# Unread matmuls at the start, page rows moved ahead of four products, pooling tiles moved into the input stage, last rows two steps sooner: a decoder trunk on one core

## The chip, the cores and the metric

The kernel runs on one core of a Trainium2 chip. The metric is the device time of one execution in microseconds, as the median of several executions. Profiled executions also give a span, from the first to the last instruction, and a trace of every engine: TensorE (PE; PEld is its weight load), VectorE (DVE), ScalarE (ACT), GpSimd (POOL) and SyncE (SP), whose queue issues all transfers here.

## The reference

One step of a two-layer decoder trunk for a prompt of 512 tokens and 8 sample sequences of 4 tokens, 544 columns in all, model width 1024. All tensors are fp32.

```
h = rmsnorm(x, g_mix);  z = h @ w_in      # one projection, split into:
    u_pool, q, kv (6 streams), nsa_gate, c_b, c_c, c_x, gate_pool, gate_nsa, gate_conv
y_pool = pool_mixer(u_pool)               # trailing means over 2/4/8/16 tokens, minus the token, then a map
y_nsa  = nsa_mixer(q, kv, nsa_gate)       # compressed + selected + windowed attention, rope on q and k
         # kv of the samples' past: cache_kv[l][page_table], 16 pages of 128 rows
y_conv = c_b * conv3(c_c * c_x)
merged = sum over b: sigmoid(gate_b) * (y_b @ w_br_b);   x = x + merged @ w_out
x = x + (silu(conv3(h2 @ W_a)) * (h2 @ W_b)) @ W_down    # h2 = rmsnorm(x, g_ffn)
after both layers: y = rmsnorm(x, norm_final)
```

## The kernel before

Activations lie transposed, 128 features by 544 columns, in tiles for each 128 features. A product tile (128 output features) is a Task in a list that is the same for both layers. It is computed in two halves of 272 columns; each half takes, for each of 8 k-tiles, three matmuls (L323, L324, L326: weight high part by input high part, high by low, low by high), 24 in all, 48 a task. A weight tile is fetched by SyncE (L306, `wr`), cast to its high part `wh` by ScalarE (L298) and its residual `wl` taken by VectorE (L299). The residual of the inputs of the first product comes from L1225. Product halves land in PSUM buffers `pg` of which there are three; a task's `evac` reads them.

The order on TensorE is the order in which the program is written. The other engines' orders are laid out by the framework's scheduler at build time, each engine then runs its own list in order.

A layer has stages. Stage "z" (the input products) holds in this order: zkc, zvc, zks (compressed keys and values, selected keys; these three run together behind the first normalisation, `mode="norm"`), zkw (window keys), four query tiles zq, zvs, zvw, zng (attention's gates), and parts of the convolution and of the compression. Keys and queries are rotated in `z_rope`: ScalarE copies PSUM to a tile (L481), SyncE shuffles it with four transfers (L483), GpSimd multiplies (L485), VectorE multiplies and adds (L484, L486); keys are then cast by ScalarE into a stacked tile (L495). A task can carry `pre`, code emitted ahead of its evacuation or product: `pages(a)` emits `pages_some` (two transfers a page, L455, with a page number loaded from memory in SyncE, L443). All pages must be there for `cmp_split`, whose casts on ScalarE are L532 and whose residuals are L534.

Behind "z" comes attention, in which TensorE's program interleaves units of one head, one branch (selected, windowed) and one block of 128 queries with tasks of stage "fill": gates and branch products of the convolution and the pooling mixer (L1085, L1093). `self.fill` says how many microseconds of fill follow a unit. A unit is scores (L830), mask, maximum, exponent (L844, L846, L852), scaling by the gate (L859 on GpSimd), transposition on TensorE (L872) and a split (L874, L875); `head_out` (L910) multiplies by the values and, for a pair of heads, splits the result (L915, L916, L341, L342) for the branch product "n" behind the attention. The pooling tiles zpool (`pool`: `pool_mix`, then `pool_map` some half products later) stand in the fill.

At the end the last down products are summed per half of the columns (L1238, L1246); `final_rows(hf)` computes the rows' factor (L374 to L393) and multiplies (L1262 on GpSimd, L1264 on VectorE). `later(n, fn)` runs a function n half products on; `fl[1]` is that number for `final_rows(0)`.

Of the kernel before, what the change touches and what calls it, by code (L numbers as in the profile page):

```python
# [6 lines left out]
F32 = mybir.dt.float32  # L7
F32R = mybir.dt.float32r
# [8 lines left out]
NP = 512  # L17
# [199 lines left out]
class Task:  # L217
    def __init__(self, name, evac, w, x, m, pre, mode, stage, halves, keep):
        self.name, self.evac, self.w, self.x, self.m = name, evac, w, x, m
        self.pre, self.mode, self.stage, self.halves, self.keep = pre, mode, stage, halves, keep  # L220
# [1 line left out]


class Trunk:
    def __init__(self, tc, ins, outs, ctx, slots=49, work=8, fill=1.66, look=3, lag=3, np_=4, nps=2, pm=9, ng=3, raw=3, by_pool=((0, 1, 2, 3, 4, 5, 6, 7), (1, 3, 5)), fl=(2, 7, 6, 1), ys=(4.0, 3.0, 10.0, 3.0, 3.0, 3.5)):
        self.tc, self.nc, self.i, self.o = tc, tc.nc, ins, outs
        pool = lambda name, **k: ctx.enter_context(tc.tile_pool(name=name, **k))
        self.cp = pool("cp", bufs=1)
        self.wp = pool("wp", bufs=4)
        self.bp = pool("bp", bufs=3)  # L230
        self.tp = pool("tp", bufs=slots)
        self.kp = pool("kp", bufs=work)
        self.dp = pool("dp", bufs=1, space=bass.MemoryType.DRAM)
        self.sp = pool("sp", bufs=2)
        self.ps = pool("ps", bufs=1, space=bass.MemoryType.PSUM)
        self.n = 0
        self.ng, self.raw = ng, raw
        self.by_pool, self.fl, self.ys_ = by_pool, fl, ys
        self.np_, self.nps, self.pm = np_, nps, pm
        self.fill, self.look, self.lag = fill, look, lag  # L240


    def nm(self, p):
# [155 lines left out]
    def setup(self):  # L399
        nc, i = self.nc, self.i  # L400
        self.cst = self.cp.tile([128, CS_W], F32, name="cst")
        self.norms = self.cp.tile([128, NM_W], F32, name="norms")
        self.ones = self.cp.tile([128, 2], F32, name="ones")
        self.vc = self.cp.tile([128, 256], F32R, name="vc").rearrange("p (g n) -> p g n", g=2)
        self.cT = self.cp.tile([128, 512], F32R, name="cT")
        self.ptt = self.cp.tile([1, 16], I32, name="ptt")
        self.cst1 = self.cst2 = None
        nc.vector.memset(self.ones, 1.0)
        nc.scalar.activation(self.ones[:, 1:2], self.ones[:, 0:1], AF.Tanh)
        self.x = [self.T() for _ in range(KT)]  # L410
        self.ident = self.c("ident")
        nc.gpsimd.memset(self.vc[64:128].bitcast(F32), 0.0)
        nc.gpsimd.memset(self.cT[64:128].bitcast(F32), 0.0)
        s, v, g = nc.scalar, nc.vector, nc.gpsimd
        by = ((s, None), (s, v), (g, None), (s, v), (s, v), (g, g), (s, v), (s, v))
        ap = self.tl[0].w[0]
        r = self.raw_weights(8)
        for t, a in ((self.norms, i["norms"]), (self.x[0], i["xT"][:, 0]), (r[:, 0:4], ap[:, 0:4]),
                     (self.x[1], i["xT"][:, 1]), (r[:, 4:8], ap[:, 4:8])):
            nc.sync.dma_start(t, a)  # L420
        for k in range(2, 7):
            nc.sync.dma_start(self.x[k], i["xT"][:, k])
        self.norm_tile(0, 0, "g_in")
        w = self.weight_parts(r, 0, 4)
        self.norm_tile(1, 0, "g_in")
        self.got[0] = w + self.weight_parts(r, 4, 8)
        self.nxt = 1
        for k in range(2, 7):
            self.norm_tile(k, 0, "g_in")
        for k in range(3):  # L430
            self.square_sum(self.x[k], k, *by[k])
        self.ahead(2)
        nc.sync.dma_start(self.x[7], i["xT"][:, 7])
        nc.sync.dma_start(self.cst, i["cst"])
        nc.sync.dma_start(self.ptt, i["pt"])
        for u in range(3, 7):
            self.square_sum(self.x[u], u, *by[u])
        self.norm_tile(7, 0, "g_in")
        self.square_sum(self.x[7], 7, *by[7])
# [522 lines left out]
    def tasks(self, l):  # L962
        nc, i = self.nc, self.i
# [3 lines left out]
        def add(name, evac, w, x=h, m=128, pre=None, mode=None, stage="rest", halves=(0, 1), keep=None):  # L967
            T.append(Task(f"{name}.{l}", evac, w, x, m, pre, mode, stage, halves, keep))

        def zt(m):  # L970
            return (i["w_in"][l, m], 8)
# [31 lines left out]
        def raw_kv(j):  # L1003
            def evac(ps):
                if j == 0:
                    nc.gpsimd.tensor_mul(self.cosr, self.cosr, self.r)
                    nc.gpsimd.tensor_mul(self.sinr, self.sinr, self.r)
                z = self.z_raw(ps)
                store("kvT", j, z)
                self.cmp_prompt(j, z)  # L1010
            return evac

        add("zkc", raw_kv(0), zt(0), pre=begin, mode="norm", stage="z")
        add("zvc", raw_kv(1), zt(1), stage="z")
        pages = lambda a: lambda: self.pages_some(l, range(a, min(a + 3, 16)))

        def rope_k(name, out, j, off, e0):
            def evac(ps):
                z = self.z_rope(ps)
                store(out, j, z)  # L1020
                setattr(self, name, self.k_stack(z, off))
                nc.gpsimd.tensor_copy(self.E[:, :, e0:e0 + 4], self.seq4(z))
            return evac

        add("zks", rope_k("ksel", "kvT", 2, 32, 16), zt(2), pre=pages(0), stage="z")
        add("zkw", rope_k("kwin", "wT", 0, 0, 20), zt(3), pre=pages(3), stage="z")

        def rope_q(r):
            def evac(ps):
# [2 lines left out]
                    self.sample_prep()  # L1032
            return evac

        for r in range(4):
            add("zq", rope_q(r), zt(4 + r), pre=pages(6 + 3 * r), stage="z")

        def raw_v(name, out, j, e0):
            def evac(ps):
# [61 lines left out]
                    nc.gpsimd.tensor_add(self.mg[m], self.mg[m], t)  # L1101
            return evac

        def pool(j):
            def evac(ps):
                pd = self.pool_mix(j, ps)
                for hf in range(2):
                    self.later(self.pm + hf, lambda hf=hf: self.pool_map(j, pd, hf))
            return evac

        kinds = {"c": (18, 0, lambda: self.yc), "p": (26, 2, lambda: self.yp), "n": (34,)}
        seq = [(key, m) for key in "cp" for m in range(8)]
        for n, (key, m) in enumerate(seq + [("n", 0)]):
            if n == 6:
                for j in range(2):
                    add("zpool", pool(j), zt(16 + j), stage="fill")
            add("gate", gate(key, m), zt(kinds[key][0] + m), stage="fill")
            if n > 0:
                key, m = seq[n - 1]
                k0, x = kinds[key][1:]  # L1120
                add("branch", branch(key, m), (i["br_a"][l, m, :, k0:k0 + 2], 2), x=x, stage="fill")
# [303 lines left out]
```

## Time and profile before

| | |
|---|---|
| median of three runs | 1762.97 us (1758.93, 1762.97, 1764.65) |
| profiled execution, its own time | 1759.85 us |
| its span | 1758.0 us |
| mean granted TensorE clock | 0.993 of full speed |
| busy: TensorE, VectorE, ScalarE, GpSimd | 1710.2, 1145.0, 737.2, 487.4 us |

An engine's busy time counts its instructions, not its waits. In a timeline a row gives the start and the duration of one instruction or of several merged, and in brackets the idle time of the engine ahead of it and what ended it. The granted clock 1.00 stands for 2.4 GHz and 0.50 for 1.2 GHz.

### The profile page before, as it was taken

What the parts mean: (1) busy time and instruction counts of PE and PEld (TensorE: products, weight loads), DVE (VectorE), ACT (ScalarE), POOL (GpSimd) and SP (SyncE); (2) the same over time, 40 slices, a digit from 0 to 9 for tenths busy, and PEclk for the clock granted to TensorE, in tenths of its full rate; (3) what the DMA queues carried; (4) which work ended last, traced back from release to release, by engine and by line L of the source; (5) the groups of instructions that cost most, each with busy time, mean ns of one, the idle gap of its engine ahead of it and who ended that gap; (6) DMA issues with size and microseconds to landing.
All of it is one profiled execution on the core that took longest, in us unless ns stands there. A gap on an engine that the chain in (4) does not pass through costs nothing.

```text
span 1758.0 us, 35101 instructions
## 1 busy us (share of the span) xinstructions
PE 1710.2 (97%) x13488; PEld 1689.6 (96%) x13488; DVE 1145.0 (65%) x2552; ACT 737.2 (42%) x1499; POOL 487.4 (28%) x719
## 2 busy tenths in 40 slices
PE   8999989999999999999998998999999999999996
PEld 8999989999999999999998998999999999999996
DVE  6675888856566565565857568887564665565566
ACT  5443555643333233233435345666333333232333
POOL 3212655630122121121231226456001321121113
PEclk9999999999999999999999999999999999999998
DMA  6653211224222322322465532112242222323322
GB/s 216 178 183 113 68 47 46 64 78 150 89 85 74 107 77 86 100 77 77 152 176 148 186 116 49 46 49 64 78 153 90 86 83 91 91 79 97 91 75 78
DMA packets 97208, 175.52 MB, mean 100 GB/s; under 512 B 31250, under 2 KB 51858, under 8 KB 97042
## 3 DMA queue, kind: packets, MB, share of 16 engines
q1 hardware_dynamic: 97042, 173.29, 32.5%
q8 instruction: 107, 1.75, 0.4%
q14 instruction: 59, 0.48, 0.1%
HBM read 157.19 MB, written 12.71 MB: 97 GB/s over the span
## 4 chain that ended last, share of the span: by engine, by line
PE 87%; DVE 7%; SPq 2%; DMA 2%; ACT 1%; issue 1%; POOL 0%; DVEq 0%; ACTq 0%; POOLq 0%
PE pg L323 25%; PE pg L324 25%; PE pg L326 25%; PE ps L830 2%; PE po L910 2%; PE pt L872 2%; SPq L483 1%; SPq L455 1%; DVE mx L846 1%; PE ps L323 1%; PE ps L324 1%; PE ps L326 1%; PE ps L1328 1%; PE ps L1329 1%; PE ps L1330 1%
## 5 line engine op out<-in xcount | busy, mean ns | idle before, releaser
L323 PE MATMUL pg<-t,wh 128*128 128x272 f32 x3824 | 1122.1, 294 | 19.8 <-DVE t L1093 8.3
L324 PE MATMUL pg<-t,wh 128*128 128x272 f32 x3824 | 1104.5, 289 | 0.7 <-DVE t L1225 0.7
L326 PE MATMUL pg<-t,wl 128*128 128x272 f32 x3792 | 1097.3, 289 | 0.0
L323 PEld LDWEIGHTS pg<-t,wh 128*128 128x128 f32 x3824 | 722.7, 189 | 24.6 <-DVE t L1093 8.8
L324 PEld LDWEIGHTS pg<-t,wh 128*128 128x128 f32 x3824 | 723.2, 189 | 2.4 <-DVE t L1225 1.0
L326 PEld LDWEIGHTS pg<-t,wl 128*128 128x128 f32 x3792 | 718.1, 189 | 0.2 <-DVE wl L299 0.2
L298 ACT CAST wh<-wr 128x512 fp32r<-128x512 f32 (+2 forms) x528 | 316.8, 602 | 581.8 <-PE pg L324 464.1
L299 DVE TENSOR_TENSOR wl<-wr,wh 128x512 fp32r<-128x512 f32 (+2 forms) x432 | 299.9, 696 | 164.8 <-ACT wh L298 146.3
L1139 DVE TENSOR_TENSOR t<-t,pg 128x272 f32<-128x272 f32 x204 | 89.1, 437 | 99.4 <-PE pg L326 97.6
L1176 POOL TENSOR_TENSOR W<-W,W 128x512 f32<-128x512 f32 x44 | 78.1, 1776 | 229.6 <-ACT wh L298 200.7
L299 POOL TENSOR_TENSOR wl<-wr,wh 128x512 fp32r<-128x512 f32 (+1 forms) x96 | 114.7, 1197 | 70.1 <-ACT wh L298 64.0
L616 POOL COPY t<-W 128x2 f32<-128x2 f32 x44 | 9.9, 225 | 369.6 <-DVE W L1159 333.0
L859 POOL TENSOR_SCALAR P<-P,ls,gate 128x128 f32<-128x128 f32 (+3 forms) x128 | 79.9, 625 | 95.7 <-DVE ls L857 61.4
L852 ACT ACTIVATE P<-ps,mx 128x256 f32<-128x256 f32 (+1 forms) x144 | 71.4, 498 | 45.7 <-DVE mx L846 33.2
L342 DVE TENSOR_TENSOR t<-W,t 128x544 fp32r<-128x544 f32 x48 | 34.9, 727 | 81.2 <-ACT t L341 81.1
L363 POOL TENSOR_TENSOR t<-t,W 128x544 f32<-128x544 f32 x19 | 26.6, 1399 | 207.4 <-ACT W L354 207.4
L874 ACT CAST b<-pt 128x128 fp32r<-128x128 f32 (+3 forms) x128 | 54.0, 422 | 49.7 <-PE pt L872 49.0
L875 DVE TENSOR_TENSOR b<-pt,b 128x128 fp32r<-128x128 f32 (+3 forms) x128 | 62.0, 485 | 16.6 <-ACT b L874 14.9
L830 PE MATMUL ps<-t,Q 128*128 128x288 f32 (+6 forms) x288 | 64.0, 312 | 4.7 <-ACT P L852 3.6
L341 ACT CAST t<-W 128x544 fp32r<-128x544 f32 x48 | 31.1, 647 | 87.0 <-POOL W L1177 82.5
L846 DVE TENSOR_REDUCE mx<-ps 128x1 f32<-128x256 f32 (+1 forms) x144 | 64.5, 448 | 2.3
L1166 ACT ACTIVATE W<-W 128x560 f32<-128x560 f32 x44 | 29.6, 673 | 74.8 <-DVE W L606 74.8
(254 smaller groups left out, 1833.5 us busy)
## 6 DMA issues: line engine op xcount, KB each, us to landing
wr<-up SPq DMA_DIRECT2D x88, 512.0 KB, 3.6
wr<-w_in SPq DMA_DIRECT2D x83, 512.0 KB, 3.8
wr<-down SPq DMA_DIRECT2D x64, 256.0 KB, 2.7
wr<-w_out SPq DMA_DIRECT2D x16, 512.0 KB, 3.6
wr<-down SPq DMA_DIRECT2D x32, 192.0 KB, 2.4
t<-xT SPq DMA_DIRECT2D x16, 272.0 KB, 5.7
b<-pgA SPq DMA_DIRECT2D x64, 64.0 KB, 2.7
wr<-cw SPq DMA_DIRECT2D x8, 512.0 KB, 3.7
```

The costliest lines, as they stand in the source:

```text
L298: nc.scalar.copy(h, r[:, k0:k1])
L299: (eng or nc.vector).tensor_sub(w, r[:, k0:k1], h)
L323: self.nc.tensor.matmul(p[:m, :HF], wh, xh[:, cs], start=a, stop=False)
L324: self.nc.tensor.matmul(p[:m, :HF], wh, xl[:, cs], start=False, stop=b and wl is None)
L326: self.nc.tensor.matmul(p[:m, :HF], wl, xh[:, cs], start=False, stop=b)
L830: nc.tensor.matmul(p[:, :n], q[:, 128 * i:128 * i + 128], kd[:, c0:c0 + n], start=u == 0, stop=u == 1)
L846: nc.vector.tensor_reduce(mx[:, u:u + 1], p[:, c0:c0 + m], axis=AX.X, op=OP.max, negate=True)
L852: nc.scalar.activation(t[:, pos:pos + m], p[:, c0:c0 + m], AF.Exp, bias=mx[:, 0:1], accum_out=ls[:, u:u + 1])
L859: nc.gpsimd.tensor_scalar(t[:, 0:n], t[:, 0:n], ls[:, 0:1], self.gate[:, i, 1 + kk, hd:hd + 1], op0=OP.mult, op1=OP.mult)
L875: nc.vector.tensor_sub(blk(pt)[:, lo][:, ::-1], blk(p)[:, 0:i + 1], blk(pt)[:, hi])
L1139: self.halves(ps, lambda p, cs: nc.vector.tensor_add(self.x[m][:, cs], self.x[m][:, cs], p))
L1176: nc.gpsimd.tensor_mul(f[:, 0:NP], t[:, 0:NP], z[:, 0:NP])
```

## The change

It does four things. Ten matmuls of 128 x 512 on a tile of ones, whose result is not read, go ahead of the first product. The pages, which were begun three at a time ahead of six tasks from zks to the fourth zq, are begun four at a time ahead of zvc, zks, zkw and the first zq. The two zpool tasks move from the fill (ahead of the seventh gate) to between the second and the third zq. And `final_rows(0)` is run 5 instead of 7 half products on.

```diff
-    def __init__(self, ..., fl=(2, 7, 6, 1), ys=...):
+    def __init__(self, ..., fl=(2, 5, 6, 1), warm=10, ys=...):
...
         self.ident = self.c("ident")
+        warm = self.W(NP, F32R)
+        nc.vector.memset(warm.bitcast(F32), 1.0)
+        p = self.PT()
+        for _ in range(self.warm):
+            nc.tensor.matmul(p, warm[:, 0:128], warm, start=True, stop=True)
...
-        add("zvc", raw_kv(1), zt(1), stage="z")
-        pages = lambda a: lambda: self.pages_some(l, range(a, min(a + 3, 16)))
+        pages = lambda a: lambda: self.pages_some(l, range(a, a + 4))
+
+        add("zvc", raw_kv(1), zt(1), pre=pages(0), stage="z")
...
-        add("zks", rope_k("ksel", "kvT", 2, 32, 16), zt(2), pre=pages(0), stage="z")
-        add("zkw", rope_k("kwin", "wT", 0, 0, 20), zt(3), pre=pages(3), stage="z")
+        add("zks", rope_k("ksel", "kvT", 2, 32, 16), zt(2), pre=pages(4), stage="z")
+        add("zkw", rope_k("kwin", "wT", 0, 0, 20), zt(3), pre=pages(8), stage="z")
...
         for r in range(4):
-            add("zq", rope_q(r), zt(4 + r), pre=pages(6 + 3 * r), stage="z")
+            if r == 2:
+                for n in range(2):
+                    add("zpool", pool(n), zt(16 + n), stage="z")
+            add("zq", rope_q(r), zt(4 + r), pre=pages(12) if r == 0 else None, stage="z")
...
         for n, (key, m) in enumerate(seq + [("n", 0)]):
-            if n == 6:
-                for j in range(2):
-                    add("zpool", pool(j), zt(16 + j), stage="fill")
             add("gate", gate(key, m), zt(kinds[key][0] + m), stage="fill")
```

Lines behind the added ones have numbers that are 5 higher; L1109 is the branch evacuation L1093, L486 is the PSUM copy L481, L500 the key cast L495, L537 the cast L532, L877, L835, L910 and L915 are L872, L830, L905 and L910.

The first place is ScalarE's list in the input products of layer 0. In the kernel before, t_488 is the rotated tile of the selected keys and t_601 that of the window keys; W_712 and W_817 take the copies of the first and the second query tile, wr_506 is the seventh weight tile and wr_619 the eighth:

```order
L298 CAST wh_508<-wr_506 128x512
L495 CAST t_499<-t_488 64x512
L495 CAST t_502<-t_488 64x512
L298 CAST wh_512<-wr_506 128x512
L481 COPY W_712<-pg_687 128x272
L481 COPY W_817<-pg_767 128x272
L495 CAST t_612<-t_601 64x512
L495 CAST t_615<-t_601 64x512
L298 CAST wh_621<-wr_619 128x512
L298 CAST wh_625<-wr_619 128x512
L481 COPY W_817<-pg_792 128x272
```

In the changed kernel, the same place; t_556 and t_680 are the rotated keys, W_802 and W_874 take the copies of the first and the second query tile, wr_574 and wr_698 are the seventh and eighth weight tiles, wr_814 that of the third query tile:

```order
L298 CAST wh_576<-wr_574 128x512
L298 CAST wh_580<-wr_574 128x512
L500 CAST t_567<-t_556 64x512
L500 CAST t_570<-t_556 64x512
L486 COPY W_802<-pg_752 128x272
L486 COPY W_802<-pg_777 128x272
L298 CAST wh_700<-wr_698 128x512
L298 CAST wh_704<-wr_698 128x512
L500 CAST t_691<-t_680 64x512
L500 CAST t_694<-t_680 64x512
L486 COPY W_874<-pg_824 128x272
L537 CAST b_1522<-b_240 128x326 x8
```

Both copies of the first query tile now stand behind the key casts, those of the second behind the casts of the eighth weight tile and of the window keys; the eight casts of `cmp_split` follow ahead of the weights of the third query tile.

The second place is TensorE's list at the end of layer 0's attention. In the kernel before, pg_5474 is a half product of fill, and po_5509 the output of the last head:

```order
L872 MATMUL pt_5496<-cst,P_5422 128x128 x4
L323 MATMUL pg_5474<-t_139,wh_5151 128x272
L324 MATMUL pg_5474<-t_140,wh_5151 128x272
L326 MATMUL pg_5474<-t_139,wl_5152 128x272
L323 MATMUL pg_5474<-t_143,wh_5151 128x272
L324 MATMUL pg_5474<-t_144,wh_5151 128x272
L326 MATMUL pg_5474<-t_143,wl_5152 128x272
L905 MATMUL po_5509<-cT,vc 128x512
```

In the changed kernel the last rows of fill (pg_5422) and those that follow are:

```order
L326 MATMUL pg_5422<-t_192,wl_5007 128x272
L877 MATMUL pt_5489<-cst,P_5345 128x128 x3
L835 MATMUL ps_5495<-t_694,Q_5135 128x384
L835 MATMUL ps_5495<-t_694,Q_5136 128x384
L877 MATMUL pt_5506<-cst,P_5394 128x128 x4
L835 MATMUL ps_5513<-t_694,Q_5135 128x512
L835 MATMUL ps_5513<-t_694,Q_5136 128x512
L877 MATMUL pt_5525<-cst,P_5450 128x128
L877 MATMUL pt_5529<-cst,P_5478 128x128 x2
L901 MATMUL pt_5534<-cst,cm_5141 32x128 x4
L877 MATMUL pt_5541<-cst,P_5502 128x128 x3
L877 MATMUL pt_5547<-cst,P_5520 128x128 x4
```

The fill that stood between the transpositions, and 24 rows of it behind head_out (pg_5537 in the kernel before), are gone from here.

The third place is SyncE's list behind the selected keys' shuffles. In the kernel before (the tile W_600 takes the window keys' shuffle; each ISA row moves a page number):

```order
L455 ISA
L455 DMA b_228<-pgA 128x2x64
L483 DMA W_600<-W_599 32x544 x4
L306 DMA wr_619<-w_in 128x1024
L974 DMA kvT<-t_488 128x544
```

In the changed kernel W_679 takes the window keys' shuffle:

```order
L460 DMA b_241<-pgA 128x2x64
L979 DMA kvT<-t_556 128x544
L488 DMA W_679<-W_678 32x544 x4
L306 DMA wr_698<-w_in 128x1024
L448 TENSOR_LOAD ptt
L448 ISA x2
```

Ahead of these rows, and behind the stores that open the stage, the kernel before has five page transfers, four shuffles and six page transfers; the changed one has 15, four shuffles and eight.

## Rows read from the trace of the kernel before

**Rows 1.** The page: busy time, share of the span and instructions of each engine.

```profile
PE 1710.2 (97%) x13488; PEld 1689.6 (96%) x13488; DVE 1145.0 (65%) x2552; ACT 737.2 (42%) x1499; POOL 487.4 (28%) x719
```

**Rows 2.** Waits of TensorE: us in total, times, longest.

```profile
PE pg L323 <- DVE t L1093: 8.3, 2, 4.2
```

**Rows 3.** Timeline of TensorE: rows with idle time ahead of them.

```profile
5.98 0.59 PE L323 MATMUL pg<-t,wh 128*128 128x272 f32 x1 [5.98 <-ACT wh L298]
...
75.23 0.34 PE L323 MATMUL pg<-t,wh 128*64 128x272 f32 x1 [1.82 <-DVE wh L318]
...
89.20 0.42 PE L700 MATMUL pt<-cst,W 24*128 24x24 f32 x4 [3.34 <-DVE W L693]
...
232.05 0.60 PE L323 MATMUL pg<-t,wh 128*128 128x272 f32 x1 [4.16 <-DVE t L1093]
...
942.12 0.34 PE L323 MATMUL pg<-t,wh 128*64 128x272 f32 x1 [1.98 <-DVE wh L318]
...
955.23 0.42 PE L700 MATMUL pt<-cst,W 24*128 24x24 f32 x4 [2.47 <-DVE W L693]
...
1097.24 0.39 PE L323 MATMUL pg<-t,wh 128*128 128x272 f32 x1 [4.13 <-DVE t L1093]
```

**Rows 4.** Four stretches: length; busy PE, PEld, DVE, ACT, POOL; clock; DMA share; GB/s.

```profile
5.90:15.75 9.85, 9.07 (x37) 8.53 (x38) 9.10 (x10) 9.10 (x16) 5.13 (x4) 1.00 0.91 356
30.80:60.80 30.00, 30.00 (x243) 30.00 (x242) 19.92 (x26) 13.37 (x26) 12.52 (x19) 1.00 0.65 172
90.90:94.30 3.40, 3.40 (x15) 3.40 (x14) 3.40 (x8) 3.40 (x6) 0.00 (x0) 0.50 0.32 94
220.00:240.00 20.00, 15.84 (x102) 15.32 (x101) 16.51 (x47) 8.88 (x24) 12.14 (x16) 0.83 0.13 36
```

**Rows 5.** Timeline of VectorE, start.

```profile
8.82 6.11 DVE L1225 SCALAR_TENSOR_TENSOR t<-t,norms,t 128x544 fp32r<-128x544 f32 x5
```

**Rows 6.** Timeline of SyncE's issues, input products of layer 0.

```profile
31.18 2.75 SPq L455 DMA_DIRECT2D b<-pgA  x5
34.03 2.52 SPq L483 DMA_DIRECT2D W<-W  x4
...
43.27 0.53 SPq L306 DMA_DIRECT2D wr<-w_in  x1
...
59.42 4.41 SPq L455 DMA_DIRECT2D b<-pgA  x6
```

**Rows 7.** Transfers issued from 29 to 77 us: KB each, median us to landing.

```profile
wr<-w_in SPq DMA_DIRECT2D x4, 512.0 KB, 4.2
b<-pgA SPq DMA_DIRECT2D x31, 64.0 KB, 2.7
W<-W SPq DMA_DIRECT2D x24, 68.0 KB, 2.0
```

**Rows 8.** Timeline of GpSimd, input products of layer 0.

```profile
39.95 1.36 POOL L485 TENSOR_TENSOR W<-W,t 128x544 f32<-128x544 f32 x1 [3.60 <-DMA W<-W]
```

**Rows 9.** Timeline of ScalarE, input products of layer 0.

```profile
47.34 1.26 ACT L495 CAST t<-t 64x512 fp32r<-64x512 f32 x2 [0.84 <-DVE t L486]
...
71.09 2.95 ACT L532 CAST b<-b 128x326 fp32r<-128x326 f32 x4 [7.36 <-DMA b<-pgA]
```

**Rows 10.** Timeline of TensorE, end of layer 0's attention.

```profile
360.76 0.64 PE L830 MATMUL ps<-t,Q 128*128 128x512 f32 x2
...
368.26 2.70 PE L910 MATMUL po<-b,t 128*128 128x128 f32 x16
```

**Rows 11.** Timeline of VectorE, end of layer 0's attention.

```profile
373.01 0.73 DVE L342 TENSOR_TENSOR t<-t,t 128x544 fp32r<-128x544 f32 x1 [0.71 <-ACT t L341]
```

**Rows 12.** Timeline of GpSimd, end of the program.

```profile
1740.75 6.17 POOL L1262 TENSOR_TENSOR W<-t,W 128x272 f32<-128x272 f32 x8 [5.49 <-ACT W L396]
```

**Rows 13.** Timeline of VectorE, end of the program.

```profile
1745.55 0.67 DVE L381 SCALAR_TENSOR_TENSOR nt<-ny 128x3 f32<-128x3 f32 x1
...
1747.17 0.16 DVE L381 SCALAR_TENSOR_TENSOR nt<-ny 128x3 f32<-128x3 f32 x1
```

More of the change, by code (lines that the diff above doesn't have):

```diff
@@ L224, with __init__ @@
 class Trunk:
-    def __init__(self, tc, ins, outs, ctx, slots=49, work=8, fill=1.66, look=3, lag=3, np_=4, nps=2, pm=9, ng=3, raw=3, by_pool=((0, 1, 2, 3, 4, 5, 6, 7), (1, 3, 5)), fl=(2, 7, 6, 1), ys=(4.0, 3.0, 10.0, 3.0, 3.0, 3.5)):
+    def __init__(self, tc, ins, outs, ctx, slots=49, work=8, fill=1.66, look=3, lag=3, np_=4, nps=2, pm=9, ng=3, raw=3, by_pool=((0, 1, 2, 3, 4, 5, 6, 7), (1, 3, 5)), fl=(2, 5, 6, 1), warm=10, ys=(4.0, 3.0, 10.0, 3.0, 3.0, 3.5)):
         self.tc, self.nc, self.i, self.o = tc, tc.nc, ins, outs
@@ L239, in __init__ @@
         self.np_, self.nps, self.pm = np_, nps, pm
-        self.fill, self.look, self.lag = fill, look, lag
+        self.fill, self.look, self.lag, self.warm = fill, look, lag, warm
     def nm(self, p):
@@ L1033, in rope_q, with pool, evac @@
             return evac
+        def pool(j):
+            def evac(ps):
+                pd = self.pool_mix(j, ps)
+                for hf in range(2):
+                    self.later(self.pm + hf, lambda hf=hf: self.pool_map(j, pd, hf))
+            return evac
         for r in range(4):
-            add("zq", rope_q(r), zt(4 + r), pre=pages(6 + 3 * r), stage="z")
+            if r == 2:
+                for n in range(2):
+                    add("zpool", pool(n), zt(16 + n), stage="z")
+            add("zq", rope_q(r), zt(4 + r), pre=pages(12) if r == 0 else None, stage="z")
         def raw_v(name, out, j, e0):
@@ L1102, in branch @@
             return evac
[L1104 to L1109, printed above, removed]
         kinds = {"c": (18, 0, lambda: self.yc), "p": (26, 2, lambda: self.yp), "n": (34,)}
```

## The prediction, made before the changed kernel ran

> **What bounds the kernel now.** I read the page's busy times first: TensorE is busy in 97% of the span [rows 1], so the end moves with TensorE's waits, its clock and the work given to it. The list of who waited for whom comes next [rows 2]: its largest entry is 8.3 us in two pieces for the branch evacuation (L1093). Third, TensorE's timeline places the waits [rows 3]: 5.98 us at the start, 1.82 and 3.34 us behind layer 0's input products, 4.16 us inside its attention, and 1.98, 2.47, 4.13 us at the same places of layer 1. Fourth, stretches with their matmul counts [rows 4]. From 30.8 to 60.8 us five products of 48 matmuls fill 30.00 us without a hole, so a half product costs 3.0 us and a matmul 0.125 us; but the first 37 matmuls take 9.07 us, 0.245 each. Behind the 3.34 us wait the granted clock reads 0.50, which is 1.2 GHz, for 3.4 us (15 matmuls, 0.227 each): half of that, 1.7 us, is lost. Between 220 and 240 us it reads 0.83: 20 x 0.17 / 0.5 = 6.8 us at half rate, of which some 1.3 us fall into the 4.16 us wait itself; the rest costs 5.5 / 2 = 2.75 us. Behind the 1.82 and 2.47 us waits I charge no clock.
>
> **The sum is made against the profiled execution's own 1759.85 us**, 3.1 us below the median 1762.97 of the three runs.
>
> **The change, part by part.**
>
> *Ten unread matmuls in front.* TensorE stands idle for its first 5.98 us [rows 3]. Ten matmuls of 512 columns cost 0.43 us each at the half-rate price (0.227 x 512 / 272), 4.3 us, and need one memset before them, so they fit. If the first product then ran at full rate, 37 matmuls at 0.125 instead of 0.245 us would give 4.4 us. But the product is fed by the residual halves (L1225) that VectorE makes, five of them in 6.11 us, the last at 14.93 us [rows 5], and every k-tile needs its own. TensorE cannot finish the last of these k-tiles before 14.93 us, and the slow stretch ends at 15.75: 0.8 us at half rate, 0.4 us, are to be had. Bounds -4.4 and +0.5 (a late memset); I take **-0.4**. The Trainium skill (TensorE: Matmul & The Clock Gate, Part 1) says that the throttled clock is the default and sustained activity releases it; by that the slow start is the clock alone, and the sum would hold -4.4. The granted clock in this case reads 1.00 from 5.9 to 15.75 us, so the trace does not bear that out.
>
> *Pages in front of products two to five.* The 32 page transfers stay 32, but more go out earlier on SyncE's queue, which is almost full there [rows 6]: five page issues take 2.75 us, four rotary shuffles 2.52 us, and six page issues whose page numbers must be loaded too 4.41 us. Today five pages stand ahead of the shuffles of the selected keys, issued at 34.03 us; now 15 do. Ten more at 0.55 us put those shuffles at 39.5 us, 5.5 us late. They land in 2.0 us, a page in 2.7, weights in 4.2 [rows 7], and their product on GpSimd (L485) starts 3.4 us behind the last issue today, at 39.95 us [rows 8]. I take 2.0: 42.0 + 2.0, then 1.36 us for L485, an estimated 0.7 for the sum behind it on VectorE (half of L485) and 1.26 for two casts on ScalarE [rows 9]: 47.4 us. ScalarE runs in program order, and the order of the changed kernel puts q0's PSUM copies behind those casts. The second half of q1 needs the buffer that the first of them frees, at 45.8 us, and gets it at 47.8: **2.1 us late**, where nobody waits today.
>
> *Pooling tiles behind the second query product.* The lateness repeats one step on. The window keys' shuffles go out behind eight more pages at 46.8 us, the eighth weight tile (43.27 us today [rows 6]) at 49.6; it lands 4.2 us later, at 53.8. Its two casts and those of the window keys now stand ahead of q1's copies, which end at 56.6 to 57.4 us. The first pooling tile's second half wants that buffer at 54: **3.3 us late**. Then ScalarE's eight casts L537 (L532 today) wait for the last page; today they begin at 71.09 us after 7.36 us of waiting, and four take 2.95 us [rows 9]; now they stand ahead of q2's weight casts. Pages land by 60.7 us, the eight casts end at 66.6, q2's casts and residuals at 67.4: q2, wanted at 66, comes **1.4 us late**, and its second weight half 0.4 more. The second pooling tile is mixed on VectorE out of one of three product buffers, and q3's first half waits for it: by my estimate **2.4 us** (bounds 0 and a half product, 3.0). The wait at L693 shrinks from 3.34 to about **2.2 us**, since some of VectorE's residuals before it are done sooner. That is 11.8 us idle, and 2.1 us of half rate behind the two longest (1.7 measured behind 3.34), 13.9 us for 1.82 + 3.34 + 1.7 = 6.9: **+7.0**. Layer 1 has the same order on SyncE and ScalarE with a little more room at the start; I get 2.2 + 3.6 + 2.2 + 1.5 = 9.5 and 1.9 of clock for 1.98 + 2.47: **+6.9**. Bounds for both layers together: 0 (half the waits, no clock) and +20 (half rate behind every wait above 2 us).
>
> *What the pooling tiles leave.* The 4.16 us wait in layer 0's attention and its 2.75 of clock go, with 0.5 of smaller ones: **-7.4**; in layer 1 4.13, 1.7 of clock and 1.0: **-6.8**. The 96 matmuls of the two tiles (12.0 us) move; none is saved. Bounds 0, should VectorE's backlog show elsewhere in the attention, and -15.
>
> *What no longer covers the last head.* Those 96 matmuls were fill, and by the order the fill now runs out that much earlier: behind the second window block of the last head only attention's own rows stand on TensorE, down to the branch that needs its output. Today the last scores start at 360.76 us, head_out takes 2.70 us from 368.26 [rows 10], and the split of its result ends at 373.74 us [rows 11], 13.0 us later, with TensorE busy all the while. Bare of fill I take 12.8 us from the last but one scores on. TensorE has about 8 us of its own in it: the ten transposes and scores some 4.2, head_out 2.7, nine branch matmuls of earlier heads 1.1. That leaves **+4.8** in each layer; bounds +2 and +7, the upper with half rate behind it.
>
> *Last rows two half products sooner.* GpSimd's eight products of the first half run 6.17 us from 1740.75 us [rows 12]; while they do, three operations in a row of a few elements on VectorE take 0.67 us each, where the same line takes 0.16 later [rows 13]. Some 2.7 us sooner, GpSimd is through before these three, which saves 1.5 us; what then runs beside it instead is slowed a little. I take **-1.2**, bounds 0 and -2.7, the whole shift.
>
> Sum: -0.4 + 7.0 + 6.9 - 7.4 - 6.8 + 4.8 + 4.8 - 1.2 = **+7.7 us**, 1767.6 us by the profiled time and 1770.7 by the median. I forecast **1769 us**.
>
> **The rivals.**
> *It all goes through* (faster). ScalarE's copies come in time, and the input products stay without a hole but for L693. That is decided where q0's first copy ends: by 45.8 us nobody waits. For it: the first half of the 2.1 us is one landing that I guessed. Against it: ten more issues at 0.55 us are 5.5 us of queue on an engine that had none to spare. The attention gives -14.2, the tails cost 4 to 9.6, both ends give 1.6, the input stage loses nothing or gains 3: **1744 to 1754 us**.
> *It cancels.* The input stage loses half of what I say (+7): 1759.85 + 7 - 14.2 + 9.6 - 1.6 = **about 1761 us**. For it: four landings are chained above, each known to about 1 us. Against it: waits behind an in-order engine add up rather than average.
> *The start gives all of 4.4 us*, the rest as forecast: **1765 us**. Against it stand L1225's times.
> *Pages collide with weights*: 24 pages and the weights share the transfers' time, and weights land 2 us later for three products of both layers: **about 1780 us**. The share of the transfer engines is 0.65 there [rows 4], which speaks against more than that.
>
> **How the numbers follow.** The forecast with its own spread (1762 to 1776) 0.48, cancelling 0.20, all through 0.16, the start 0.08, collision 0.08. A measurement of this kernel can tell 0.3%, 5.3 us, from no change. Slower by more (above 1768.3) are the upper part of the forecast and the collision: 0.45; faster by more (below 1757.7) the all-through case and part of the cancelling one: 0.24; the rest 0.31. The range leaves out a tenth at each end: 1748 to 1781.
>
> **What would show it.** Right: waits of 2 to 3.5 us between the input products that end with a PSUM copy on ScalarE (L486), then one for q2's weights; no wait for L1109 (L1093 today) in the attention; 4 to 5 us idle behind the last scores of each layer; a first product with spacing 0.125 us, broken by waits for L1231 (L1225 today). Wrong: no wait for ScalarE's copies between 40 and 60 us, or fill up to the end of the attention.

## The result

The changed kernel takes 1771.8 us (median of six runs, 1770.81 to 1777.23) where the kernel before takes 1762.68 (six runs, 1758.10 to 1764.65): 9.1 us slower by the medians. The ratio of the means is 1.0064 (11.2 us), 95% interval 1.0046 to 1.0081, clear of 1; the ratios given for the runs below are made in the same way. The forecast was 1769 us, slower. The profiled execution of the changed kernel took 1775.18 us, 3.4 above its median, that of before 1759.85, 2.8 below its own; a comparison of the two traces therefore shows 15.3 us, 6 of which, by the medians, belong to these two executions and not to the change.

The page of the changed kernel:

```profile
span 1773.5 us, 35141 instructions
...
PE 1722.0 (97%) x13498; PEld 1696.8 (96%) x13498; DVE 1144.0 (65%) x2561; ACT 738.4 (42%) x1499; POOL 488.4 (28%) x711
```

TensorE is still busy 97% [rows 1]. Its waits (us in total, times, longest) are new ones:

```profile
PE pg L323 <- ACT W L486: 11.1, 4, 3.6
PE pt L705 <- DVE W L698: 4.4, 2, 2.2
PE pg L323 <- DVE pf L650: 4.1, 2, 2.4
```

Nobody waited for a PSUM copy on ScalarE (L481, now L486) before; that is now the largest entry, 11.1 us in four pieces. The entry for the branch evacuation (8.3 us) [rows 2] is gone. TensorE's timeline, rows with idle time ahead of them, is the answer to [rows 3]:

```profile
49.53 0.40 PE L323 MATMUL pg<-t,wh 128*128 128x272 f32 x1 [3.59 <-ACT W L486]
...
58.22 0.60 PE L323 MATMUL pg<-t,wh 128*128 128x272 f32 x1 [2.44 <-ACT W L486]
...
75.28 0.60 PE L323 MATMUL pg<-t,wh 128*128 128x272 f32 x1 [2.21 <-DVE W L648]
...
81.67 0.36 PE L323 MATMUL pg<-t,wh 128*128 128x272 f32 x1 [1.71 <-DVE pf L650]
...
114.80 0.42 PE L705 MATMUL pt<-cst,W 24*128 24x24 f32 x4 [2.22 <-DVE W L698]
...
376.70 0.63 PE L877 MATMUL pt<-cst,P 128*128 128x128 f32 x4 [1.15 <-DVE cT L904]
...
921.93 0.40 PE L323 MATMUL pg<-t,wh 128*128 128x272 f32 x1 [1.51 <-ACT W L486]
...
931.73 0.59 PE L323 MATMUL pg<-t,wh 128*128 128x272 f32 x1 [3.52 <-ACT W L486]
```

In the input products of layer 0 there are five waits where there was one (the fifth, 0.44 us at 69.32, isn't shown), and three in layer 1 (the third, 2.41 us at 950.95, isn't shown either); in the attention there is none of 4 us, but the last head has several (376.70 is the longest). The stages are measured between rows that both kernels have (the norm's L393, the gates' L700 or L705, the next norm). With the pooling tiles 13.8 us of work moved in each layer: 96 matmuls at 0.125 us, and the four products of `pool_map` (L684, before L679), which the trace shows as two rows each and which take 0.45 us from start to start:

```profile
100.20 0.62 PE L684 MATMUL ps<-W,t 128*128 128x272 f32 x2
100.66 0.60 PE L509 MATMUL pt<-cst,W 128*128 128x128 f32 x4
```

Less these 13.8 us, the two executions differ as follows:

| stage | before, us | after, us | difference without the moved work | predicted |
|---|---|---|---|---|
| start to the norm | 27.32 | 27.22 | -0.1 | -0.4 |
| input products, layer 0 | 61.88 | 87.58 | +11.9 | +8.7 |
| attention to the next norm, layer 0 | 403.39 | 385.26 | -4.3 | -4.3 |
| feed-forward, layer 0 | 401.42 | 401.59 | +0.2 | 0 |
| input products, layer 1 | 61.22 | 84.07 | +9.1 | +6.9 |
| attention to the next norm, layer 1 | 402.38 | 387.73 | -0.9 | -2.0 |
| from there to the first half's L374 | 375.70 | 375.69 | 0 | 0 |
| end | 24.69 | 24.36 | -0.3 | -1.2 |

(The 1.7 us of half rate behind layer 0's gates [rows 4], which the predicted +7.0 for the input products takes off, lie behind the row that ends this stage; in the table they are taken off the attention: +8.7 and -4.3 in place of +7.0 and -2.6.)

SyncE's queue and ScalarE's list show why the input products are late:

```profile
31.28 4.28 SPq L460 DMA_DIRECT2D b<-pgA  x7
...
36.27 5.20 SPq L460 DMA_DIRECT2D b<-pgA  x8
41.56 2.51 SPq L488 DMA_DIRECT2D W<-W  x4
...
51.72 0.58 SPq L306 DMA_DIRECT2D wr<-w_in  x1
```

```profile
47.81 1.26 ACT L500 CAST t<-t 64x512 fp32r<-64x512 f32 x2 [4.34 <-DVE t L491]
49.09 0.68 ACT L486 COPY W<-pg 128x272 f32<-128x272 f32 x2
55.47 1.14 ACT L298 CAST wh<-wr 128x512 fp32r<-128x512 f32 x2 [5.70 <-DMA wr<-w_in]
...
57.79 0.67 ACT L486 COPY W<-pg 128x272 f32<-128x272 f32 x2
62.23 6.13 ACT L537 CAST b<-b 128x326 fp32r<-128x326 f32 x8 [3.76 <-DMA b<-pgA]
68.65 1.14 ACT L298 CAST wh<-wr 128x512 fp32r<-128x512 f32 x2 [0.30 <-DMA wr<-w_in]
```

Fifteen page issues stand ahead of the selected keys' shuffles, which go out at 41.56 us where they went out at 34.03 [rows 6]. Their casts end at 49.07 and the copies of the first query tile follow at 49.09: TensorE goes on at 49.53. The eighth weight tile, issued at 51.72 instead of 43.27, is cast at 55.47, and the copies behind it release TensorE at 58.22. The eight casts L537 wait for the last page until 62.23 and hold the next weights until 68.65. For the shuffles and the eighth tile it is the issue that is late, not the landing: those shuffles still land in 2.0 us (median), the tile in 3.6 us where it took 4.5.

### The profile page after: what moved, and what is told of

Read it like the earlier page. It is cut to its first block, busy times and chain, and to the rows that moved or that the text cites. A ratio compares the mean times of both kernels' runs of the same rounds, so it can differ in the third digit from the quotient of the medians.

```text
span 1773.5 us, 35141 instructions
## 1 busy us (share of the span) xinstructions
PE 1722.0 (97%) x13498; PEld 1696.8 (96%) x13498; DVE 1144.0 (65%) x2561; ACT 738.4 (42%) x1499; POOL 488.4 (28%) x711
## 4 chain that ended last, share of the span: by engine, by line
PE 91%; DVE 4%; DMA 2%; ACT 1%; SPq 1%; issue 1%; POOL 0%; DVEq 0%; ACTq 0%; POOLq 0%
PE pg L323 26%; PE pg L324 26%; PE pg L326 26%; PE po L915 2%; PE ps L835 2%; PE pt L877 2%; DMA wr<-w_in 1%; PE ps L326 1%; PE ps L324 1%; PE ps L323 1%; PE ps L1334 1%; PE ps L1335 1%; PE ps L1336 1%; DVE wl L299 1%; SPq L488 0%
## 5 line engine op out<-in xcount | busy, mean ns | idle before, releaser
L323 PE MATMUL pg<-t,wh 128*128 128x272 f32 (+1 forms) x3824 | 1121.1, 293 | 21.6 <-ACT W L486 11.1
L324 PE MATMUL pg<-t,wh 128*128 128x272 f32 (+1 forms) x3824 | 1103.8, 289 | 2.3 <-DVE t L1231 1.4
L323 PEld LDWEIGHTS pg<-t,wh 128*128 128x128 f32 (+1 forms) x3824 | 721.7, 189 | 27.5 <-ACT W L486 11.9
L324 PEld LDWEIGHTS pg<-t,wh 128*128 128x128 f32 (+1 forms) x3824 | 722.5, 189 | 4.5 <-DVE t L1231 2.2
L299 DVE TENSOR_TENSOR wl<-wr,wh 128x512 fp32r<-128x512 f32 (+1 forms) x440 | 308.0, 702 | 180.0 <-ACT wh L298 160.7
L299 POOL TENSOR_TENSOR wl<-wr,wh 128x512 fp32r<-128x512 f32 (+1 forms) x88 | 102.7, 1171 | 22.2 <-ACT wh L298 20.2
L835 PE MATMUL ps<-t,Q 128*128 128x288 f32 (+6 forms) x288 | 62.9, 308 | 2.9 <-ACT P L857 2.7
```

What stands on the lines that cost most here:

```text
L299: (eng or nc.vector).tensor_sub(w, r[:, k0:k1], h)
L323: self.nc.tensor.matmul(p[:m, :HF], wh, xh[:, cs], start=a, stop=False)
L324: self.nc.tensor.matmul(p[:m, :HF], wh, xl[:, cs], start=False, stop=b and wl is None)
L835: nc.tensor.matmul(p[:, :n], q[:, 128 * i:128 * i + 128], kd[:, c0:c0 + n], start=u == 0, stop=u == 1)
```

## The experiments

Each run was timed in five rounds beside the kernel before on the same chip.

**Which part costs.** First the two large parts, one undone at a time.

```diff
-            if r == 2:
-                for n in range(2):
-                    add("zpool", pool(n), zt(16 + n), stage="z")
...
+            if n == 6:
+                for j in range(2):
+                    add("zpool", pool(j), zt(16 + j), stage="fill")
```

> The changed kernel with the two pooling tiles back in the fill; unread matmuls, early pages and early last rows stay. If the early pages alone make the shuffles and with them the copies late (my theory), the wait of some 3.5 us for q0's copies at 49.5 us stays, one of about 2 for q1's too, and each layer's input products lose about 4 us against the kernel before, while the attention has its wait of 4 us back and its last head is covered: 1768 us. If the pooling tiles are what makes the input products wait (rival), the early pages cost nothing: 1761 us.

1774.75 us, ratio 1.0058 (1.0043 to 1.0072). The early pages alone make the kernel slower by as much as the whole change; the copies are late without any pooling tile near them:

```profile
49.96 0.59 PE L323 MATMUL pg<-t,wh 128*128 128x272 f32 x1 [4.09 <-ACT W L486]
...
68.64 0.40 PE L323 MATMUL pg<-t,wh 128*128 128x272 f32 x1 [3.35 <-ACT W L486]
```

The wait at 49.96 is the one of the changed kernel, that at 68.64 the copy behind L537; the branch's wait is back with 4.14 us at 241.71. My sum of 4 us a layer for the early pages was too small.

```diff
-        pages = lambda a: lambda: self.pages_some(l, range(a, a + 4))
-        add("zvc", raw_kv(1), zt(1), pre=pages(0), stage="z")
+        pages = lambda a: lambda: self.pages_some(l, range(a, min(a + 3, 16)))
+        add("zvc", raw_kv(1), zt(1), stage="z")
...
-            add("zq", rope_q(r), zt(4 + r), pre=pages(12) if r == 0 else None, stage="z")
+            add("zq", rope_q(r), zt(4 + r), pre=pages(6 + 3 * r), stage="z")
```

> The changed kernel with the pages begun three at a time in front of six tasks as before; the pooling tiles stay in the input products. My theory: the shuffles go out at 34 us again, no wait for the copies L486 between 45 and 60 us, so 3.6 + 2.4 us and their half-rate clock (1.7) go in layer 0 and 5 + 1.7 in layer 1; what stays are the waits behind the pooling tiles' evacuation: about 1759 to 1762 us. Rival: the pooling tiles alone make the waits, and the time stays at 1770 us.

1770.42 us, 1.0038 (1.0024 to 1.0053). The early waits for copies are gone as expected, but the time is the rival's figure, 8 us or more above mine, for a reason I had not counted:

```profile
85.51 0.59 PE L323 MATMUL pg<-t,wh 128*128 128x272 f32 x1 [5.19 <-ACT W L486]
...
948.12 0.60 PE L323 MATMUL pg<-t,wh 128*128 128x272 f32 x1 [6.62 <-ACT W L486]
```

```profile
79.57 5.61 ACT L537 CAST b<-b 128x326 fp32r<-128x326 f32 x8 [6.77 <-DMA b<-pgA]
85.08 0.38 ACT L486 COPY W<-pg 128x272 f32<-128x272 f32 x1
```

Pages that are begun ahead of the third and fourth query tile are now begun behind 12 us of pooling products, L537 waits for the last of them until 79.57, and a copy stands behind it in ScalarE's order: one wait of 5.2 us in layer 0 and of 6.6 in layer 1. So each of the two large parts costs by itself (10.9 and 6.6 us by the medians), together 9.1: the costs don't add. Both runs have a wait in layer 0 for a copy that stands behind L537 on ScalarE (68.64 and 85.51); that they don't add because of such shared lateness is argued, not shown.

**The small parts.**

```diff
-        warm = self.W(NP, F32R)
-        nc.vector.memset(warm.bitcast(F32), 1.0)
...
-            nc.tensor.matmul(p, warm[:, 0:128], warm, start=True, stop=True)
```

> The changed kernel without the ten unread matmuls and their memset. The trace of the changed kernel shows the norm's first matmul 0.1 us sooner than before, though its first matmuls ran at full rate: 1772 us, no difference (within 2 us). Rival: they gave what the half-rate start cost, 4.4 us, and without them it is 1776 us.

1775.6 us, 1.0072 (1.0054 to 1.0090). The rival's 1776 us would be 0.25% over the changed kernel, at the edge of this interval, so that this run alone doesn't rule it out.

```diff
-    def __init__(self, ..., fl=(2, 5, 6, 1), ...):
+    def __init__(self, ..., fl=(2, 7, 6, 1), ...):
```

> The changed kernel with the last rows of the first half 7 instead of 5 half products on, as before. The profile of the changed kernel has its last 25 us 0.3 us shorter than the one before: 1772 us, no measurable difference. My prediction had 1.2 us for it, 1773 us; the rival, that the whole shift counts, 1774.5 us.

1774.22 us, 1.0062 (1.0047 to 1.0077). Neither differs from the changed kernel's 1.0064. The two alone, put on the kernel before:

> The kernel before with the two small parts alone: ten unread matmuls in front and the last rows 5 half products on; pages and pooling tiles as before. From the profiles of the changed kernels (0.1 us at the norm, 0.3 us at the end) and the runs without either part: no difference from the kernel before, 1762 us; my prediction had 1.6 us for the two, 1761. Rival, each gives its whole: 1756 us.

1761.38 us, 0.9993 (0.9980 to 1.0006): no difference, as expected. A gain of 4.4 us at the start would be 0.9975, outside the interval.

**Where the lateness comes from.** The pages of the third to fifth product go behind that product's shuffles:

```diff
-        def rope_k(name, out, j, off, e0):
+        def rope_k(name, out, j, off, e0, pg):
             def evac(ps):
                 z = self.z_rope(ps)
+                pg()
...
```

> The changed kernel with the pages of the third to fifth product put behind that product's shuffles in the program instead of ahead of it; the number of pages and all else stay. My theory: the selected keys' shuffles go out near 36 us instead of 41.6, the copies of the first two query tiles come in time, the waits for L486 (3.6 + 2.4 us in layer 0, 1.5 + 3.5 in layer 1) and two half-rate stretches go: 12 us less than the changed kernel, 1759 to 1762 us. Rival: it is the amount of page traffic, not its place, that makes the copies late: no difference from the changed kernel, 1772 us.

1773.04 us, 1.0067 (1.0051 to 1.0083). My theory, that the pages' place ahead of the shuffles is the fault, falls. The copies are late by only 1.08 us, and the weights by more instead:

```profile
52.94 0.40 PE L323 MATMUL pg<-t,wh 128*128 128x272 f32 x1 [1.08 <-ACT W L486]
...
59.28 0.39 PE L323 MATMUL pg<-t,wh 128*128 128x272 f32 x1 [3.08 <-ACT wh L298]
```

```profile
37.28 2.52 SPq L488 DMA_DIRECT2D W<-W  x4
...
52.60 0.42 SPq L306 DMA_DIRECT2D wr<-w_in  x1
```

The shuffles go out at 37.28, but the eighth weight tile at 52.60, behind the third group of pages (eight transfers from 47.65 on, 4.38 us), and TensorE waits 3.08 us for its cast. This tile also lands more slowly than in either kernel (4.5 us before, 3.6 in the changed one):

```profile
wr<-w_in SPq DMA_DIRECT2D x1, 512.0 KB, 5.9
```

So it arrives 10.7 us later than before the change: 9.3 us of that are issue, 1.4 us landing. The time is the rival's figure (the amount of page traffic), and this run doesn't separate the queue's time from the transfers'. The same with the pooling tiles back in the fill, by the edit of the first run:

> Shuffles ahead of the pages and the pooling tiles back in the fill (unread matmuls and early last rows stay). My theory: the input products are back to the two waits of the kernel before, the attention too; start and end give 0.4 us: 1762 to 1763 us, as the kernel before. Rival (amount of page traffic): 1772 us as with the pooling tiles in the fill and the pages ahead.

1780.72 us, 1.0111 (1.0092 to 1.0129), the slowest of all: waits for weights of 2.86 and 3.31 us in layer 0, 2.41 and 1.91 in layer 1, and the attention's 4 us again. In both orders something that stands behind the early pages is late. So the pages were taken in fewer issues, four pages of one half a transfer:

```diff
-        for j in js:
-            v = self.page(j)
-            for st in range(2):
-                nc.sync.dma_start(self.cb[st][:, :, 64 * j:64 * j + 64], ...)
+        a = js[0]
+        for st in range(2):
+            for g in range(2):
+                nc.sync.dma_start(self.cb[st][:, g, 64 * a:64 * a + 256].rearrange("p (o n) -> p o n", o=4),
+                                  self.i["pgA"][l, a:a + 4, :, st, g].rearrange("o p n -> p o n"))
```

> The changed kernel with four pages fetched by four transfers instead of eight, and without page numbers (it fetches pages 0 to 15 in their order, so the compressed keys and values of the samples are those of other pages): the same bytes by half the issues on SyncE, at the same places in the program. Theory now: SyncE's time per issue is what makes everything behind the pages late, shuffles or weights, whichever stands behind; with half the issues no wait for L486 or for weights over 1 us is left before the pooling tiles' own: 1760 to 1764 us. Rival: it is the bytes, landing slower while pages run: 1772 us.

1753.78 us, 0.9951 (0.9933 to 0.9970): faster than both kernels, but without the page list it computes something else, so it says what the issues cost and is no candidate. In the input products no wait for a copy or for weights is left, only those for the pooling tiles' evacuation:

```profile
PE pg L323 <- DVE pf L650: 4.5, 4, 1.6
PE pt L705 <- DVE W L698: 4.5, 2, 2.2
```

```profile
7.62 5.86 SPq L460 DMA_DIRECT2D b<-pgA  x5
...
14.14 1.53 SPq L460 DMA_DIRECT2D b<-pgA  x3
```

The queue's rows show that the run doesn't separate two things: with no page numbers to wait for, eight of the sixteen transfers went out from 7.62 to 15.67 us, ahead of the input products, so there are fewer issues there for both reasons. With them half of the layer's page bytes left the input products too, so the run doesn't rule out the rival (bytes) either.

With page numbers and 32 transfers a layer as before, the issues were put where the queue has room: layer 0's first three pages in the setup, its other thirteen in front of products three to six (three, three, three and four), and all of layer 1's ahead of layer 0's feed-forward. The pooling tiles stay where the change has them.

```diff
+        self.pages_cmp(0)
+        self.pages_some(0, range(3))
...
         def begin_ffn():
+            if l == 0:
+                self.pages_cmp(1)
+                self.pages_some(1, range(16))
...
-        pages = lambda a: lambda: self.pages_some(l, range(a, a + 4))
+        pages = lambda a: lambda: self.pages_some(l, range(a, min(a + 3, 16) if a < 12 else 16)) if l == 0 else None
...
-            add("zq", rope_q(r), zt(4 + r), pre=pages(12) if r == 0 else None, stage="z")
+            add("zq", rope_q(r), zt(4 + r), pre=pages(9 + 3 * r) if r < 2 else None, stage="z")
```

> The changed kernel with the same 32 page transfers a layer, but put where SyncE's queue has room: layer 0's first three pages in the setup and the rest three at a time behind the first two query tiles' tasks at the latest, layer 1's all ahead of layer 0's feed-forward products. Pooling tiles, unread matmuls and last rows as in the changed kernel. Theory (SyncE's queue in the input products is the bound): no wait for the copies or for weights above 1 us in layer 1, at most one in layer 0, input products 2 to 4 us a layer over the kernel before, the attention keeps its gain: 1754 to 1758 us, faster than both. Rival (the pooling tiles' own waits eat what the attention gains): 1763 us.

1763.03 us, 1.0007 (0.9996 to 1.0018): 9 to 10 us better than the changed kernel, but no gain on the kernel before. The time is the rival's (the pooling tiles' own waits), but the loss lies in layer 0 alone. From norm to norm layer 1 takes 460.5 us where it took 463.6 before, layer 0 471.6 where it took 465.3.

```profile
66.02 0.60 PE L323 MATMUL pg<-t,wh 128*128 128x272 f32 x1 [6.18 <-DVE W L650]
```

VectorE's rows ahead of it, and the row of GpSimd that they waited for:

```profile
59.69 0.72 DVE L493 TENSOR_TENSOR t<-t,W 128x544 f32<-128x544 f32 x1 [4.83 <-POOL W L492]
61.52 1.29 DVE L299 TENSOR_TENSOR wl<-wr,wh 128x512 fp32r<-128x512 f32 x2 [1.10 <-ACT wh L298]
62.73 2.78 DVE L824 SCALAR_TENSOR_TENSOR Q<-t,Q 64x512 fp32r<-64x512 f32 x4
65.52 0.44 DVE L650 TENSOR_TENSOR W<-pg,t 128x272 f32<-128x272 f32 x1
```

```profile
58.28 1.38 POOL L492 TENSOR_TENSOR W<-W,t 128x544 f32<-128x544 f32 x1 [6.78 <-DMA W<-W]
```

In layer 1, whose pages are all there, the input products have no wait over 0.6 us up to the gates': the change's attention gain is kept there. In layer 0 a wait of 1.72 us for a copy (53.59) and one of 6.18 us remain, the longer for VectorE's first operation on the first pooling tile (L650, L648 in the changed kernel). It stands behind two weight residuals and four splits of a query; VectorE waited for GpSimd until 59.69, and GpSimd 6.78 us for the first query tile's shuffles, which SyncE issued from 53.55 us on, behind pages of layer 0. So this wait, too, goes back to the queue. A place for layer 0's pages and pooling tiles without such a wait was not found.

**The last head.** The fill per unit was cut so that it lasts:

```diff
-    def __init__(self, ..., fill=1.66, ...):
+    def __init__(self, ..., fill=1.45, ...):
```

> The changed kernel with 1.45 instead of 1.66 us of fill behind a unit of attention, so that fill lasts beyond the last head_out again. My theory: the waits of the last head (3.4 us in layer 0, 3.0 in layer 1, and some 2.5 us of half rate) go: about 5 us less than the changed kernel, 4 above the kernel before (1767 to 1768 us). Rival: less fill in the middle opens waits there (the scores' waits of 0.4 to 1 us multiply), and nothing is won.

1778.65 us, 1.0101 (1.0081 to 1.0120): worse. The waits of the last head go, and waits further ahead in the attention appear, as the rival says, 8.3 us of them for the scaling factor (L862), for which TensorE did not wait in the changed kernel:

```profile
PE pt L901 <- DVE ls L862: 8.3, 6, 1.6
```

That edit and the order of the shuffles above, together:

> Both edits together: shuffles ahead of the pages, and 1.45 us of fill. If each term stands alone they add: 1754 to 1757 us, faster than the kernel before. If fill was worth nothing: as with the shuffles alone.

1776.53 us, 1.0085 (1.0067 to 1.0103): as the fill alone says, and not the sum that I expected.

**Another place for the pooling tiles**, behind zvw, with the pages begun as before the change:

```diff
...
         for r in range(4):
-            if r == 2:
-                for n in range(2):
-                    add("zpool", pool(n), zt(16 + n), stage="z")
...
         add("zvw", raw_v("vwin", "wT", 1, 20), zt(9), stage="z")
+        for n in range(2):
+            add("zpool", pool(n), zt(16 + n), stage="z")
```

> The changed kernel with the pages as before and the pooling tiles behind the last value tile (zvw) and ahead of the attention's gates instead of between the query tiles. Theory now: the input products up to zvw run as in the kernel before, the 12 us of pooling products cover ScalarE's wait for the last page (7.4 us) that ends in the 1.8 and 2.0 us waits, the attention keeps its 7 and 3 us (tails deducted): 1753 to 1757 us, faster than both. Rival: VectorE's mixing of the pooling tiles makes its residuals and L698 later by as much as the attention gains: 1762 us.

1770.29 us, 1.0045 (1.0029 to 1.0061). The rival was nearer than my theory, and too low; the wait for L698 that it names is shorter than before (0.9 us in each layer). Layer 0 has waits of 3.5 us for the first pooling tile's evacuation and of 1.2 for the second's; moving the tiles down moves the waits down.

## Why the prediction came out

**The input products** were the step that decided, and the kind of wait is shown: TensorE waits for the copies on ScalarE, then for the weights, then for the second pooling tile on VectorE, as the prediction says. For layer 0 it had 2.1, 3.3, 1.8, 2.4 and 2.2 us; measured are 3.59, 2.44, 0.44, 2.21 + 1.71 and 2.22, 12.6 in place of 11.8. The sum is near, but partly by luck: the wait for the third query tile's weights is 1.4 us shorter than said, and the one for the second pooling tile 1.5 us longer, most of it (2.21 us, L648) half a product sooner than said. In layer 1 the waits are 1.51, 3.52, 2.41, 2.21 for the predicted 2.2, 3.6, 2.2, 1.5.

The size of the term was short all the same, +8.7 against +11.9 in layer 0 and +6.9 against +9.1 in layer 1 for this pair of executions, most of it because of the clock. I had charged 2.1 us of half rate for layer 0, and there are two stretches of it in the input products, none of them behind the longest wait:

```profile
49.50:55.70 6.20, 6.17 (x48) 6.03 (x48) 1.40 (x3) 0.50 (x2) 1.61 (x2) 1.00 0.68 202
57.80:61.20 3.40, 2.98 (x13) 2.98 (x14) 2.09 (x4) 0.66 (x2) 0.00 (x0) 0.52 0.31 68
74.90:78.30 3.40, 3.02 (x13) 3.02 (x14) 3.31 (x8) 0.12 (x1) 0.65 (x1) 0.52 0.69 205
```

Two stretches of 3.4 us at a clock of 0.52 lose 3.3 us. In layer 1 there are two as well, from 931.7 and from 952.1 us on, where I had charged 1.9 us. A third stretch in layer 0 follows the gates' 2.22 us wait, as one did before. The rest is small: 0.8 us of waits in layer 0, and some 0.16 us for each of four more waits, since a matmul's row lasts 0.29 us where the next one starts 0.125 us later when nothing is waited for. The step that gave the lateness of the shuffles (5.5 us) was 2 us short: a page took 0.61 to 0.65 us to issue here and not 0.55, and one of the two stores now stands between the pages (35.67 us) and no longer ahead of them.

What the prediction had too narrow is the cause. It laid the lateness to shuffles that stand behind pages; with the order reversed the weights are late instead. In the changed kernel's trace it is the queue's time: the shuffles and the eighth weight tile are issued 7.5 and 8.5 us late and land as fast as before. With the order reversed slower landing adds to it.

**The attention's gain** came: no wait of 4 us is left. The waits of the last head come to 4.3 us in layer 0 and 4.0 in layer 1 for the predicted 4.8; in layer 1 the granted clock also fell, to a mean of 0.56 from 1245 to 1252 us. Net -4.3 and -0.9 for -4.3 and -2.0.

**The start.** The unread matmuls take 4.63 us for the 4.3 costed and end at 6.1 us. From the first product's fourth matmul on the rows show the full rate:

```profile
6.83 0.29 PE L323 MATMUL pg<-t,wh 128*128 128x272 f32 x1
...
7.86 0.39 PE L324 MATMUL pg<-t,wh 128*128 128x272 f32 x1 [0.36 <-DVE t L1231]
...
10.53 0.60 PE L324 MATMUL pg<-t,wh 128*128 128x272 f32 x1 [1.02 <-DVE t L1231]
...
10.20:13.60 3.40, 3.07 (x13) 3.07 (x14) 3.40 (x4) 3.40 (x7) 3.04 (x2) 0.50 1.01 410
```

TensorE then waits twice for VectorE's residuals (L1231, L1225 before) and once, at 9.12 us, for ScalarE (L1230), and runs at half rate again from 10.2 to 13.6 us. The limit of 14.93 us [rows 5] held; the rival of 4.4 us is out, by this trace and by the run of the two small parts alone. The Trainium skill's rule (TensorE: Matmul & The Clock Gate, Part 1: activity releases the throttled clock) agrees with the rate from 6.83 us on, 0.125 us a matmul; what it would have given was never TensorE's to take. The prediction's objection to that rule was a misreading: the granted clock reads 1.00 there in the kernel before, but its rows are those of the half rate, 0.23 us from start to start as behind the 3.34 us wait [rows 4], and not 0.125:

```profile
8.23 0.43 PE L326 MATMUL pg<-t,wl 128*128 128x272 f32 x1
```

**The end.** The three slow steps did fall outside GpSimd's shadow, and the wait ahead of the last L393 fell from 4.07 to 2.51 us. But GpSimd's products now run beside four of VectorE's sums instead of two:

```profile
1756.07 1.85 DVE L1252 TENSOR_TENSOR t<-t,W 128x272 f32<-128x272 f32 x2
...
1758.76 1.71 DVE L1252 TENSOR_TENSOR t<-t,W 128x272 f32<-128x272 f32 x2
...
1762.13 0.16 DVE L381 SCALAR_TENSOR_TENSOR nt<-ny 128x3 f32<-128x3 f32 x1
```

1.85 and 1.71 us for two sums, where one alone takes 0.44 us; before, one pair was slowed so (1.84 us, at 1741.60), now two are. The row of the kernel before:

```profile
1741.60 1.84 DVE L1246 TENSOR_TENSOR t<-t,W 128x272 f32<-128x272 f32 x2
```

So the factor's chain began later: its steps are short now, 0.16 us as the last of [rows 13], and what they gained was mostly given back to the sums, with a new wait of 0.69 us at 1754.03 and L374's of 2.69 in place of 2.38 us: -0.3 for -1.2.

**Not settled:** how the 9.1 us of the medians divide over the stages, since one execution of each kernel was profiled and such executions differ by 6 us. In this pair the terms come to 15.5 us for the forecast 7.7, so that part of the nearness of 1769 to the median is luck. Also open: how the lateness divides over issuing and landing where the pages stand behind the shuffles, and what transfers of several pages would give with page numbers that are read from the list, since the run with fewer issues changed both.

## What to carry to other kernels

A queue that issues for everybody is a resource of its own: count its issues per stage, at their measured time, ahead of asking what stands behind what. Here reordering inside a full queue only chose who was late, and page issues moved to a stage where the queue idles took the lateness away in layer 1; that fewer issues in the same place would do so is likely, but not shown alone. Work that is moved out of a filler stage leaves a hole at its end and brings its evacuation with it, and both have to be priced against the wait that it leaves behind.

## What the hardware showed that I had not expected

The length of a wait alone didn't tell whether TensorE's clock falls behind it. In the changed kernel a wait of 3.59 us (49.53) was followed by 6.2 us at granted clock 1.00, while waits of 2.44 and 2.21 us were followed by 3.4 us at 0.52. In the run without the unread matmuls the same place had a wait of 3.41 us, and the granted clock behind it was 0.50 for 3.5 us:

```profile
49.50:53.00 3.50, 3.43 (x15) 3.43 (x16) 0.40 (x1) 0.30 (x2) 0.00 (x0) 0.50 0.60 175
```

And at the start of the changed kernel 2.88 us of work in 4.30 us, in pieces, were followed by half rate, though no single wait up to the row at 10.53 us was longer than 1.02 us. At the very start the record of the granted clock was no guide to the rate: in the kernel before it reads 1.00 from 5.9 us on, while rows 0.23 us apart show the half rate.
